# Last squares of an RMS norm: summed on VectorE, or as extra products on TensorE

## Chip, cores and metric

The kernel runs on one NeuronCore of one Trainium2 chip. The metric is device time in microseconds (us) of one launch. Three runs of the kernel before took 983.26, 982.51 and 980.66 us, so the median is 982.51 us.

## What is computed

The reference is a block of two layers on 256 tokens of width 1024. Each layer has an RMS norm, one wide projection, three kinds of attention, gated branch projections, an output projection, a second RMS norm, an MLP of width 4096, a third RMS norm and a gated projection of a side input. What matters here is the norm and where its result goes:

```python
def rmsnorm(x, g):
    xf = x.astype(jnp.float32)
    y = xf * lax.rsqrt(jnp.mean(xf * xf, axis=-1, keepdims=True) + EPS)
    return (y * g.astype(jnp.float32)).astype(x.dtype)
...
        h = rmsnorm(x, attn_norm[i])
        proj = h @ w_in[i]
...
        hm = rmsnorm(x, mlp_norm[i])
        x = x + jnp.square(jax.nn.relu(hm @ w_up[i])) @ w_down[i]

        hp = rmsnorm(x, ple_norm[i])
        x = x + jax.nn.sigmoid(hp @ w_ple_gate[i]) * (p[i] @ w_ple_proj[i])
```

## The kernel before

**Layout.** The residual `xT` lies transposed: 128 features on the partitions, 8 feature tiles, 256 tokens along the row. Each fp32 operand of a large product is split into a high and a low part (`split`, L458, for activations; `load_unit`, L393, for weights: a copy on ScalarE gives `wh`, a subtraction on VectorE or GpSimd gives `wl`), and TensorE forms three products per tile (`mm3`, L412). Weights arrive in units of 512 KB through the one queue of SyncE; a unit's buffer `w` comes free, and the next load is issued, when its `wl` has been made.

**The norm.** `class Norm` (L483) works on `xT` as its tiles are finished, two feature tiles at a time. `add` (L495) writes the two parts `xh`, `xl` of x times the gain, and has ScalarE square the two tiles into `sq`. The squares are summed over the feature tiles into one tile `ssum` (128 features by 256 tokens): GpSimd (POOL) does that for the first three pairs, VectorE (DVE) for the last pair, in two additions that follow each other (L509). `end` (L511) sums over the 128 partitions on TensorE (PE): for each of the two blocks of 128 tokens, one product with `ssum` as the 128x128 stationary operand and a column of -1 as the moving one, into `nps`. Then DVE makes `ms` (mean plus epsilon), POOL takes the power -1/2 (`rsq`), and where a row form is wanted (`row`, L522) DVE builds a diagonal `dg`, PE spreads it over the partitions (`rps`) and ScalarE (ACT) copies it to `rrow`. The large products on the unnormalised `xh`, `xl` do not wait for any of this: only what evacuates them from PSUM does, since rstd is applied there.

There are five norms that take this path (the very first sums otherwise). In the order of time: the MLP norm of layer 0 (the **first** in what follows), its gate norm (`ple`, the **second**), the attention norm of layer 1 (the **third**), the MLP norm of layer 1 (the **fourth**) and its gate norm (the **fifth**).

**The order of the work.** Nothing is issued directly. `Program` records every operation with its dependences, a cost from a table (`price`, L171) and a priority, which is the running sum of TensorE's costs where the operation was written, minus a lead for loads and weight splits. `schedule` (L218) then plays a list scheduler over the five engines on these estimates and writes down one order per engine; the chip runs each engine's list strictly in that order. All instructions therefore carry L293, the line that emits them. A new operation or another cost can shift the order of anything behind it. An engine that reaches an instruction whose input is not there yet waits, with everything behind it.

PSUM tiles of the large products, `mmp`, have two buffers; `nps` and `rps` come from another pool.

Of the kernel before, what the change touches and what calls it, by code (L numbers as in the profile page):

```python
# [18 lines left out]
OP = mybir.AluOpType  # L19
# [4 lines left out]
P = 128  # L24
# [272 lines left out]
def hybrid_block(ctx: ExitStack, tc: tile.TileContext, I, out):  # L297
    nc = tc.nc
    prog = Program(nc)
    V, S, G, T, Q = (prog.engine(e) for e in ("DVE", "ACT", "POOL", "PE", "SP"))  # L300
# [24 lines left out]
    def t2k(name, cols=512):  # L325
        return prog.tile(sp, [P, cols], F32, name, tag="t2", bufs=T2, ahead=AHEAD_T2)
# [4 lines left out]
    def small(name, shape, bufs, dt=F32, tag=None):  # L331
        return prog.tile(gaps.get(name) or pool_for(shape, dt), shape, dt, name, tag=tag or name, bufs=bufs)
# [10 lines left out]
    def trp(name):  # L343
        return prog.tile(ptr, [P, 512], F32, name, tag="tr", bufs=2, ahead=1)
# [42 lines left out]
    def mm(out, lhsT, rhs, start, stop):  # L387
        T.matmul(out=out, lhsT=lhsT, rhs=rhs, start=start, stop=stop, skip_group_check=True)
# [61 lines left out]
    def rsqrt_mean(ss, n, width):  # L450

        ms = small("ms", [P, 8], 4)
        V.tensor_scalar(ms[:, :n], ss, 1.0 / width, EPS, op0=OP.mult, op1=OP.add)
        r = small("rsq", [P, 8], 10)
        G.tensor_tensor(out=r[:, :n], in0=ms[:, :n], in1=half[:, :n], op=OP.pow)
        return r[:, :n]

    def split(src, dh, dl, col=None):  # L458

        if col is None:  # L460
            S.activation(dh, src, AF.Copy)
            V.tensor_tensor(out=dl, in0=src, in1=dh.bitcast(F32), op=OP.subtract)
        else:
            S.activation(dh, src, AF.Copy, scale=col)
            V.scalar_tensor_tensor(dl, src, col, dh.bitcast(F32), op0=OP.mult, op1=OP.subtract)
# [17 lines left out]
    class Norm(Acts):  # L483
# [11 lines left out]
        def add(self, ft, square=True):  # L495
            xh, xl = self.tiles[0]
            for f in range(ft.start, ft.stop):
                split(xT[:, f, :], xh[:, f, :], xl[:, f, :], self.gains[:, f:f + 1])
            if not square:
                return  # L500
            n = ft.stop - ft.start
            sq = t2k("sq", n * SEQ).rearrange("p (f t) -> p f t", t=SEQ)
            S.activation(sq, xT[:, ft, :], AF.Square)
            if self.ss is None:
                self.ss = small("ssum", [P, SEQ], 1)
                G.tensor_tensor(out=self.ss, in0=sq[:, 0, :], in1=sq[:, 1, :], op=OP.add)
            else:
                for f in range(n):
                    (V if ft.stop == 8 else G).tensor_tensor(out=self.ss, in0=self.ss, in1=sq[:, f, :], op=OP.add)  # L509

        def end(self, ss=None):  # L511
            if ss is None:
                ps = trp("nps")
                for b in range(NB):
                    mm(ps[:, b:b + 1], self.ss[:, b * P:(b + 1) * P], negone[:, 0:1], True, True)
                r = rsqrt_mean(ps[:, 0:NB], NB, -D)
            else:
                r = rsqrt_mean(ss, NB, D)
            self.rstd = [r[:, b:b + 1] for b in range(NB)]
# [66 lines left out]
    for n in range(2):  # L586
        for b in range(NB):
            ps = trp("xps")
# [59 lines left out]
    negone = negone_r.bitcast(F32)  # L648
# [50 lines left out]
    for l in range(DEPTH):  # L699
# [362 lines left out]
        for b in range(NB):  # L1062
            ps = trp("plps")
# [73 lines left out]
```

## Time and profile before

| what | value |
|---|---|
| runs | 983.26, 982.51, 980.66 us; median 982.51 |
| profiled execution, device time | 980.81 us |
| its span, first to last instruction | 979.0 us |
| TensorE busy | 964.5 us (99%) |
| VectorE busy | 654.6 us (67%) |
| ScalarE busy | 539.1 us (55%) |
| GpSimd busy | 154.8 us (16%) |
| DMA engines busy | 55% |
| mean granted TensorE clock | 0.996 of full |

The profiled execution's span lies 1.8 us below its device time. TensorE is the engine that is never idle for long; the others are shown with their busy time only, and much of it lies beside TensorE's. A matmul's row gives a start and a modelled duration, and these overlap: what a product costs TensorE is the distance from its start to the next start, not its duration. A plain fp32 product (`nps`, `rps`) has two matmul rows, each with a weight load of its own.

### The profile page before, as it was taken

The page shows a single profiled execution, that of the slowest core. Times are in us where ns is not written, and L with a number is a line of the kernel's source. Part 1 is how long each engine was busy: PE and PEld are TensorE (multiplying, and loading weights), DVE is VectorE, ACT ScalarE, POOL GpSimd, SP SyncE. Part 2 cuts the span into 40 slices and gives each one's busy share as a digit, 9 for nine tenths or more (in the row PEclk, how much of TensorE's full clock was granted, in tenths as well). Part 3 has the DMA queues.
Part 4 walks back from the last instruction along what each step waited for, and adds up shares of the span by engine and source line. Part 5 has one row for each costly group of instructions (what it writes and reads, how often), then busy time and mean ns, then how long its engine had stood idle before and what let it go on. Part 6 is the DMA issues. An engine that isn't in the chain of part 4 may idle for free.

```text
span 979.0 us, 18465 instructions
## 1 busy us (share of the span) xinstructions
PE 964.5 (99%) x7506; PEld 909.6 (93%) x7506; DVE 654.6 (67%) x1009; ACT 539.1 (55%) x770; POOL 154.8 (16%) x137
## 2 busy tenths in 40 slices
PE   8899999999999999999999999999999999999998
PEld 7888889889999999999989888898899999999997
DVE  8748897664777554567676599975547855565573
ACT  7437674466456444556474576645745644555462
POOL 1202122314220000001312112231151200000010
PEclk9999999999999999999999999999999999999999
DMA  8664255535666656556455543556265665566651
GB/s 282 177 207 129 89 156 172 177 114 180 197 174 198 204 183 210 176 175 214 142 171 173 190 138 110 155 170 195 88 185 182 182 214 187 172 198 201 205 173 44
DMA packets 89195, 168.59 MB, mean 172 GB/s; under 512 B 5723, under 2 KB 9237, under 8 KB 89109
## 3 DMA queue, kind: packets, MB, share of 16 engines
q1 hardware_dynamic: 89108, 167.40, 55.0%
q8 instruction: 59, 0.97, 0.4%
q14 instruction: 28, 0.22, 0.1%
HBM read 166.33 MB, written 1.05 MB: 171 GB/s over the span
## 4 chain that ended last, share of the span: by engine, by line
PE 92%; DVE 3%; ACT 2%; DMA 2%; issue 1%; SPq 0%; POOL 0%; ACTq 0%; DVEq 0%
PE mmp L293 66%; PE acc L293 18%; PE z L293 2%; PE sc L293 2%; PE oc L293 1%; DMA w<-in_w_in 1%; DVE qo L293 1%; PE qps L293 1%; ACT wh L293 1%; DVE wl L293 1%; PE ob L293 1%; PE pps L293 1%; DVE io L293 1%; DMA xin<-in_x 0%; DVE rm L293 0%
## 5 line engine op out<-in xcount | busy, mean ns | idle before, releaser
L293 ACT ACTIVATE wh<-w 128x1024 fp32r<-128x1024 f32 (+2 forms) x318 | 330.9, 1045 | 204.7 <-PE mmp L293 103.4
L293 DVE TENSOR_TENSOR wl<-w,wh 128x1024 fp32r<-128x1024 f32 (+1 forms) x284 | 342.3, 1213 | 148.1 <-ACT wh L293 143.1
L293 PE MATMUL mmp<-xh,wh 128*128 128x256 f32 x1088 | 306.4, 282 | 2.6 <-DVE rm L293 2.6
L293 PE MATMUL mmp<-xh,wl 128*128 128x256 f32 x1088 | 305.5, 281 | 0.0
L293 PE MATMUL mmp<-xl,wh 128*128 128x256 f32 x1088 | 304.6, 280 | 0.0
L293 PEld LDWEIGHTS mmp<-xh,wh 128*128 128x128 f32 x1088 | 206.5, 190 | 4.9 <-ACT wh L293 3.5
L293 PEld LDWEIGHTS mmp<-xh,wl 128*128 128x128 f32 x1088 | 206.0, 189 | 1.2 <-issue 1.0
L293 PEld LDWEIGHTS mmp<-xl,wh 128*128 128x128 f32 x1088 | 205.7, 189 | 0.4
L293 PE MATMUL acc<-yh,wh 128*128 128x256 f32 x512 | 141.5, 276 | 0.0
L293 PE MATMUL acc<-yh,wl 128*128 128x256 f32 x512 | 141.3, 276 | 0.0
L293 PE MATMUL acc<-yl,wh 128*128 128x256 f32 x512 | 141.3, 276 | 0.0
L293 POOL TENSOR_TENSOR wl<-w,wh 128x1024 fp32r<-128x1024 f32 x34 | 84.1, 2473 | 214.7 <-ACT wh L293 214.7
L293 PE MATMUL mmp<-wh,xh 128*128 128x512 f32 (+2 forms) x296 | 113.2, 382 | 0.7 <-ACT av L293 0.7
L293 PE MATMUL mmp<-wh,xl 128*128 128x512 f32 (+2 forms) x296 | 112.9, 383 | 0.2 <-DVE xl L293 0.2
L293 PE MATMUL mmp<-wl,xh 128*128 128x512 f32 (+2 forms) x296 | 112.1, 380 | 0.0
L293 PEld LDWEIGHTS acc<-yl,wh 128*128 128x128 f32 x512 | 96.1, 188 | 0.0
L293 PEld LDWEIGHTS acc<-yh,wh 128*128 128x128 f32 x512 | 96.1, 188 | 0.0
L293 PEld LDWEIGHTS acc<-yh,wl 128*128 128x128 f32 x512 | 96.1, 188 | 0.0
L293 PE MATMUL mmp<-yl,wh 128*128 128x256 f32 x336 | 93.0, 278 | 0.2
L293 PE MATMUL mmp<-yh,wh 128*128 128x256 f32 x336 | 93.0, 277 | 0.2 <-ACT pp L293 0.2
L293 PE MATMUL mmp<-yh,wl 128*128 128x256 f32 x336 | 92.8, 277 | 0.0
L293 POOL TENSOR_TENSOR rsq<-ms,half 128x8 f32<-128x8 f32 (+3 forms) x30 | 47.0, 1570 | 221.4 <-DVE ms L293 221.4
(196 smaller groups left out, 1205.1 us busy)
## 6 DMA issues: line engine op xcount, KB each, us to landing
w<-in_w_in SPq DMA_DIRECT2D x118, 512.0 KB, 3.9
w<-in_w_up SPq DMA_DIRECT2D x64, 512.0 KB, 3.8
w<-in_w_down SPq DMA_DIRECT2D x64, 512.0 KB, 4.6
w<-in_w_out SPq DMA_DIRECT2D x16, 512.0 KB, 4.4
w<-in_w_ple_gate SPq DMA_DIRECT2D x16, 512.0 KB, 3.8
w<-in_w_br_a SPq DMA_DIRECT2D x8, 512.0 KB, 4.8
w<-in_w_br_c SPq DMA_DIRECT2D x8, 512.0 KB, 3.7
w<-in_w_br_b SPq DMA_DIRECT2D x8, 512.0 KB, 4.5
```

The costliest lines, as they stand in the source:

```text
L293: getattr(self.engines[op.eng], op.name)(*op.args, **op.kw)
```

## The change

`add` keeps the squares of the last two feature tiles as they are, in `rest`, and no longer adds them to `ssum`. `end` makes three products per block of tokens in place of one, accumulated in PSUM: one of `ssum`, and one of each kept square.

```diff
             S.activation(sq, xT[:, ft, :], AF.Square)
-            if self.ss is None:
+            if ft.stop == 8:
+                self.rest = [sq[:, f, :] for f in range(n)]
+            elif self.ss is None:
                 self.ss = small("ssum", [P, SEQ], 1)
                 G.tensor_tensor(out=self.ss, in0=sq[:, 0, :], in1=sq[:, 1, :], op=OP.add)
             else:
                 for f in range(n):
-                    (V if ft.stop == 8 else G).tensor_tensor(out=self.ss, in0=self.ss, in1=sq[:, f, :], op=OP.add)
+                    G.tensor_tensor(out=self.ss, in0=self.ss, in1=sq[:, f, :], op=OP.add)
 
         def end(self, ss=None):
             if ss is None:
                 ps = trp("nps")
+
+                parts = [self.ss, *self.rest]
                 for b in range(NB):
-                    mm(ps[:, b:b + 1], self.ss[:, b * P:(b + 1) * P], negone[:, 0:1], True, True)
+                    for i, q in enumerate(parts):
+                        mm(ps[:, b:b + 1], q[:, b * P:(b + 1) * P], negone[:, 0:1], i == 0, i == len(parts) - 1)
                 r = rsqrt_mean(ps[:, 0:NB], NB, -D)
```

Over the five norms DVE loses 10 additions and PE gains 20 products (40 matmul rows). The scheduler also moves what stands near. Three pieces show it.

On PE at the second norm (`mmp_952` and `mmp_953` are products of the gate's side projection, `nps_937` the norm's sum, lines with + are of the change):

```order
 L293 MATMUL mmp_952<-yl_917,wh_950 128x256
 L293 MATMUL mmp_952<-yh_916,wl_951 128x256
+L293 MATMUL nps_937<-negone_r_130,sq_936 128x1 x2
+L293 MATMUL nps_937<-negone_r_130,ssum_927 128x1
+L293 MATMUL nps_937<-negone_r_130,sq_936 128x1 x2
 L293 MATMUL mmp_953<-yh_916,wh_950 128x256
 L293 MATMUL mmp_953<-yl_917,wh_950 128x256
 L293 MATMUL mmp_953<-yh_916,wl_951 128x256
 L293 MATMUL mmp_953<-yh_916,wh_950 128x256
-L293 MATMUL nps_937<-negone_r_130,ssum_927 128x1 x2
```

The sum stands four products earlier, ahead of `mmp_953`; its first product, of `ssum` for the first block, is not in this piece and stands eight products further ahead.

On DVE at the second norm (`ssum_927` the additions, `ms_938` and `dg_940` the steps behind the sum, `wl_977` and `wl_980` splits of later weights):

```order
 L293 TENSOR_TENSOR xT_102<-acc_685,xT_102 128x512
 L293 SCALAR_TENSOR_TENSOR xl_915<-xT_102,ncol_101,xh_914 128x256
-L293 TENSOR_TENSOR ssum_927<-ssum_927,sq_936 128x256 x2
+L293 TENSOR_SCALAR ms_938<-nps_937 128x2
 L293 SCALAR_TENSOR_TENSOR xl_915<-xT_102,ncol_101,xh_914 128x256 x2
-L293 TENSOR_SCALAR ms_938<-nps_937 128x2
+L293 TENSOR_SCALAR dg_940<-ident_87,rsq_939 128x128 x2
 L293 TENSOR_TENSOR wl_977<-w_975,wh_976 128x1024
-L293 TENSOR_SCALAR dg_940<-ident_87,rsq_939 128x128 x2
 L293 TENSOR_TENSOR wl_980<-w_978,wh_979 128x1024
```

The two additions are gone, and `ms` stands in their place, ahead of the two `xl`; `dg` passes one weight split.

On PE at the third norm (`mmp_1011` and `mmp_1013` are the two blocks of the first projection of layer 1, `nps_993` the sum):

```order
+L293 MATMUL nps_993<-negone_r_130,sq_992 128x1 x2
+L293 MATMUL nps_993<-negone_r_130,ssum_971 128x1
+L293 MATMUL nps_993<-negone_r_130,sq_992 128x1 x2
 L293 MATMUL mmp_1011<-wh_1009,xl_955 128x512
-L293 MATMUL mmp_1013<-wh_1006,xh_954 128x512
-L293 MATMUL mmp_1013<-wl_1007,xh_954 128x512
-L293 MATMUL mmp_1013<-wh_1006,xl_955 128x512
-L293 MATMUL nps_993<-negone_r_130,ssum_971 128x1 x2
 L293 MATMUL mmp_1013<-wh_1009,xh_954 128x512
```

The group of five products stands one product of `mmp_1011` and six of `mmp_1013` ahead of the next tile, `mmp_1030`; before, the sum stood six products ahead of it. The first product of `ssum` stands four products of `mmp_1011` ahead of the group.

At the first and the fourth norm the first product of `ssum` stands 39 products of 256 columns ahead of where the sum stood, and the other five 23 products ahead of it, with the 16 between them. At the fifth the first stands two products into `mmp_1803`, with the sum ten products and eight transposes behind that place before; the other five stand six products of `mmp_1804` ahead of the old place, and four of the eight transposes move to a later tile.

## Rows read from the trace of the kernel before

**Rows 1.** The page: TensorE's busy time; shares of the chain that ended last.

```profile
PE 964.5 (99%) x7506; PEld 909.6 (93%) x7506; DVE 654.6 (67%) x1009; ACT 539.1 (55%) x770; POOL 154.8 (16%) x137
...
PE 92%; DVE 3%; ACT 2%; DMA 2%; issue 1%; SPq 0%; POOL 0%; ACTq 0%; DVEq 0%
```

**Rows 2.** Tile ssum: count, duration in ns (min/median/max), first and last start.

```profile
L293 PE MATMUL nps<-negone_r,ssum x20: 164/250/271, 293.2 to 951.8; 128*128 128x1 f32 x20
L293 DVE TENSOR_TENSOR ssum<-ssum,sq x10: 410/418/1709, 290.7 to 950.0; 128x256 f32<-128x256 f32 x10
```

**Rows 3.** Timeline of PE, first norm: start, duration, instruction, [idle before <-releaser].

```profile
293.03 0.28 PE L293 MATMUL mmp<-xh,wh 128*128 128x256 f32 x1
293.15 0.50 PE L293 MATMUL nps<-negone_r,ssum 128*128 128x1 f32 x4
...
293.71 0.28 PE L293 MATMUL mmp<-xh,wl 128*128 128x256 f32 x1
```

**Rows 4.** Timeline of PE, second norm.

```profile
465.99 0.28 PE L293 MATMUL mmp<-yl,wh 128*128 128x256 f32 x1
...
467.68 0.28 PE L293 MATMUL mmp<-yh,wh 128*128 128x256 f32 x1
469.01 0.61 PE L293 MATMUL nps<-negone_r,ssum 128*128 128x1 f32 x4 [1.06 <-DVE ssum L293]
...
469.68 0.36 PE L293 MATMUL mmp<-yh,wl 128*128 128x256 f32 x1
...
473.22 0.28 PE L293 MATMUL mmp<-xl,wh 128*128 128x256 f32 x1
...
473.90 0.59 PE L293 MATMUL rps<-dg,negone_r 128*128 128x256 f32 x2
474.15 0.47 PE L293 MATMUL mmp<-xl,wh 128*128 128x256 f32 x1
```

**Rows 5.** Timelines of POOL, ACT and DVE, second norm.

```profile
464.08 1.79 POOL L293 TENSOR_TENSOR ssum<-ssum,sq 128x256 f32<-128x256 f32 x2 [2.10 <-ACT sq L293]
465.83 2.39 POOL L293 TENSOR_TENSOR wl<-w,wh 128x1024 fp32r<-128x1024 f32 x1
469.90 1.63 POOL L293 TENSOR_TENSOR rsq<-ms,half 128x2 f32<-128x2 f32 x1 [1.68 <-DVE ms L293]
...
466.07 0.62 ACT L293 ACTIVATE sq<-xT 128x512 f32<-128x512 f32 x1
...
466.79 2.17 DVE L293 TENSOR_TENSOR ssum<-ssum,sq 128x256 f32<-128x256 f32 x2 [1.52 <-ACT sq L293]
```

**Rows 6.** Stretches: busy time by engine, then granted TensorE clock, DMA share, GB/s.

```profile
32.80:36.20 3.40, 3.40 (x19) 3.40 (x18) 2.24 (x8) 0.00 (x0) 0.55 (x1) 0.50 0.77 243
...
469.70:473.10 3.40, 3.40 (x18) 3.40 (x18) 2.56 (x6) 1.54 (x2) 1.63 (x1) 0.51 0.66 194
...
517.20:520.60 3.40, 3.40 (x30) 3.34 (x30) 2.83 (x9) 1.36 (x3) 0.00 (x0) 1.00 0.61 177
```

**Rows 7.** Timeline of PE: its two other waits of over one microsecond.

```profile
32.02 0.36 PE L293 MATMUL mmp<-xh,wh 128*128 128x256 f32 x1 [2.56 <-DVE rm L293]
...
517.04 0.33 PE L293 MATMUL ips<-ident,io 128*128 128x128 f32 x1 [1.62 <-DVE io L293]
```

**Rows 8.** Timelines of PE and DVE, third norm.

```profile
503.32 0.39 PE L293 MATMUL mmp<-wh,xh 128*128 128x512 f32 x1
...
504.70 0.50 PE L293 MATMUL nps<-negone_r,ssum 128*128 128x1 f32 x4
505.06 0.48 PE L293 MATMUL mmp<-wh,xh 128*128 128x512 f32 x1
...
506.95 0.41 PE L293 MATMUL mmp<-wh,xh 128*128 128x324 f32 x1 [0.26 <-ACT av L293]
...
505.23 0.16 DVE L293 TENSOR_SCALAR ms<-nps 128x2 f32<-128x2 f32 x1 [0.69 <-PE nps L293]
```

**Rows 9.** Timeline of POOL, first norm: its last additions, and the power behind the sum.

```profile
286.79 1.79 POOL L293 TENSOR_TENSOR ssum<-ssum,sq 128x256 f32<-128x256 f32 x2 [5.64 <-ACT sq L293]
293.93 0.71 POOL L293 TENSOR_TENSOR rsq<-ms,half 128x2 f32<-128x2 f32 x1 [5.35 <-DVE ms L293]
```

## Prediction

> **What bounds the kernel now.** I read the page first, to see who is never idle: TensorE (PE) is busy 964.5 of 979.0 us and holds 92% of the chain that ended last [rows 1]. What lies on PE therefore lengthens the run by its full price unless PE would have waited there anyway, and what is taken from VectorE (DVE, 67%) is worth only the wait of PE that it ends. Then I read PE's timeline around each of the five norms for waits. At the first norm there is none: the sum's products stand in an unbroken stream [rows 3]. The fourth and the fifth look the same. At the second, PE stands idle for the additions of DVE [rows 4], and the timelines of the other engines say why [rows 5]. At the third it does not wait for the sum, but a little later for what follows it [rows 8]. A table of stretches gives the clock [rows 6].
>
> **What a product costs.** In the steady stream a product of 256 columns starts 0.113 us after the one before it (473.22 to 473.90 holds six steps) [rows 4]. From 293.03 to 293.71 PE starts one such product, the four matmul rows of two `nps` products, and one more large one [rows 3]. That is 0.68 us, less 2 x 0.113 leaves 0.454, so **0.227 us** per `nps` product, or 0.113 per matmul row. One column costs as much as 256, because each row loads 128 columns of weights. The Trainium skill would price it lower: "TensorE: Matmul & The Clock Gate", section "Back-to-back issue gap", gives matmuls of 1 to 64 columns a floor of about 25 ns; at that, the 40 added rows would be an estimated 1.0 us. The measured row decides.
>
> **First, fourth and fifth norm: +0.91 us each.** Four more products by 0.227 are 0.91, and nothing is there to be won. New waits could come in two places. The first product, of `ssum`, now stands 39 products earlier than the sum did, so PE reaches it at 293.15 - 39 x 0.113 = 288.73, and POOL's last addition ends at 286.79 + 1.79 = 288.58 [rows 3, 9]: 0.15 us to spare, and I price it at nothing. If that cover is gone, each 0.1 us of lateness is 0.1 us of PE. The squares' own products stand another 16 products later. The two additions that DVE loses are 0.42 us each in ten places [rows 2]; behind them DVE splits weights and makes `ms`, on none of which PE waits here, so they are worth nothing. Moving `rps` and `rrow` forward brings no gain either, since the evacuation that uses them holds up no product. Together: +2.73.
>
> **Second norm: a gain, of a size that hangs on the clock.** ACT finishes the squares at 466.69. The first DVE addition starts at 466.79 and both end only at 468.96: POOL is splitting weights from 465.83 to 468.22, and the addition, 0.42 us elsewhere, takes up to 1.71 [rows 2, 5]. PE, whose last product started at 467.68, goes on at 469.01 [rows 4]. In the change the sum needs only the squares and POOL's additions. The first product would start at 465.99 (POOL ends at 464.08 + 1.79 = 465.87) [rows 4, 5]; eight products later, at 465.99 + 0.23 + 8 x 0.113 = 467.12, the squares have been ready for 0.4 us, and the other five run to 468.26. Work that PE does there also covers a short wait for a PSUM buffer before `mmp_953`.
>
> Before, the stretch from 465.99 to 474.15 holds 37 large products, the sum and `rps`: 8.16 us [rows 4]. After, it should hold 37 x 0.113 = 4.19, six `nps` products at 0.227 = 1.36, `rps` 0.25 (473.90 to 474.15), in all 5.80, plus a possible wait for `rps`. That one I bound: `ms` about 0.17 us after the last product and the power 0.24 after that, as at the first and third norm, so it starts at 468.67 and lasts 0.71 (DVE quiet) to 1.63 (DVE busy beside it) [rows 5, 9]; with 0.5 for `dg`, `rps` can run at 469.9 to 470.8, and PE is there at 468.26 + 18 x 0.113 = 470.3. So 0 to 0.5; I take 0.2, nearer the short one, since DVE has only two `xl` there. The stretch becomes 6.0: **-2.16**.
>
> Of this, 1.61 is clock: from 469.68 to 473.22 PE started 17 products in 3.54 us, at twice the usual step (17 x 0.113 = 1.93), and the stretch shows a granted clock of 0.51, the 1.2 GHz level [rows 4, 6]. It fell behind the wait. It also fell behind a wait of 2.56 us at 32.02 (0.50 after it), and not behind one of 1.62 us at 517.04 (1.00 after it) [rows 6, 7]. A wait of 1.06 and some idling before it is thus at the edge, and one execution doesn't say whether the others paid the 1.61. The price in the median run lies between 0 and 1.61; the longer wait that cost no clock is the nearest row, so I take 0.5. The second norm is then -0.55 - 0.5 = **-1.05**.
>
> **Third norm: +0.77.** A product of 512 columns steps by 0.23 (503.32 to 504.70 holds six) [rows 8]. The first `nps` product takes the place of a large one that now follows, so the group of five starts at about 504.70 and ends at 505.83. `mmp_1030` needs a PSUM buffer that ACT evacuates with the new rstd. From the sum's last row (before: next product at 505.06) to `ms` (505.23) are 0.17 us, and from there over POOL and ACT to `mmp_1030` (506.95) 1.72 [rows 8]. That gives 505.83 + 0.17 + 1.72 = 507.72 against 506.95: +0.77. PE arrives at 505.83 + 7 x 0.23 = 507.44, so part of the added work falls into a wait that was there already. The reordered steps of ACT and DVE ahead of this norm only bring the squares earlier; I price them at nothing, with 0.3 either way.
>
> **Sum.** 2.73 - 1.05 + 0.77 = **+2.45 us**, on the median of 982.51: **984.96**. Against the profiled execution's own time, where the clock did fall, it is 2.73 - 2.16 + 0.77 = +1.34, 982.15 from 980.81, which itself is 1.7 below the median. With no clock to win back it is +2.95. A measurement of this kernel tells about 0.3%, 2.95 us, from no change, so the forecast is "same", leaning slow.
>
> **Rivals.**
> - *New waits take the place of the old one* (slower, 30%). The wait for DVE becomes waits on POOL: for its additions, which now gate a product 39 places earlier with 0.15 us to spare, and for the power at the second norm (0.5 in place of 0.2). It decides once POOL's additions end after PE's arrival. For it: the thin cover. Against it: the same additions end at the same distance in the fourth norm. With the runs' clock unfallen before (2.95), 0.3 at `rps` and 0.2 to 0.5 at two or three norms, it is +3.65 to +4.75: 986.2 to 987.3. The unfallen clock with no new wait at all ends on the bound, and I count a third of its cases here.
> - *The new bursts lower the clock* (slower, 7%). Five one-column products are 1.13 us in which PE streams ten columns. If the chip takes that for idling, a fall costs 1.61 as at the second norm; at two to five norms that makes +5.7 to +10.5, 988.2 to 993.0. Against it: two such products in a row leave the next steps at 0.113 [rows 3]; bursts of five are not in the trace. The section on what is happening in the skill's page "TensorE: Matmul & The Clock Gate" ties the clock to how busy PE has been, without saying how one column counts; no row here shows it.
> - *Every execution before paid for the clock, and the chains move up* (faster, 3%). All of 1.61 comes back, which leaves +1.34; and the sum at the first norm ends at 288.73 + 0.23 + 16 x 0.113 + 1.13 = 291.9, 1.7 us earlier than at 293.6 [rows 3]. If PE waited on what follows at three norms, that would be another -5.1: -3.8, 978.7. Against it: no wait of PE hangs on these chains but those priced.
> - *A product at its issue floor* (2%): the added 4.54 us shrink to 1.0 and the sum is -1.1, still within 0.3%. The section cited above states that floor; rows 3 speak against it.
>
> **How the numbers follow.** Forecast 58% (+1.2 to +2.95), new waits 30%, bursts 7%, faster 3%, issue floor 2%. Faster by over 0.3%: 0.03. Within: 0.58 + 0.02 = 0.60. Slower: 0.37. The range goes from 982.0 (the profiled sum) to 987.6 (the waits at their full price and some tenths of spread); the bursts are left out.
>
> **What would show it.** DVE 10 additions fewer, about 4 us less busy; 60 `nps` matmul rows in place of 20, still at 0.113 a step. At the second norm no idle time of PE on DVE and a clock of 1.00 throughout. At the third `mmp_1030` still waiting some 0.3 us for ACT's `av`. Wrong would be: idle time of PE in front of an `nps` product with POOL or ACT as the releaser, a stretch at 0.5 behind a burst, or PE standing still elsewhere because the new order came out late.

## The result, and the profile after

The change makes the kernel slower: a median of 990.12 us over 8 runs (984.63 to 995.21) against 979.94 of the kernel before, run beside it on the same chip (8 runs, 977.81 to 983.26). The ratio is 1.0098, with a 95% interval of 1.0071 to 1.0125. The forecast was 984.96 with a range that ended at 987.6, so the time lies outside, on the slow side. It stood on 982.51, the median of the first three runs of the kernel before; of the change itself it gave +2.45 us, and +10.2 was measured. The runs of the changed kernel spread over 10.6 us, those of the kernel before over 5.5. Its profiled execution happens to be the fastest of the eight: 984.63 us, span 982.9.

The page of the changed kernel: busy time and the chain that ended last, to be read against [rows 1].

```profile
PE 967.9 (98%) x7546; PEld 913.0 (93%) x7546; DVE 648.7 (66%) x999; ACT 540.0 (55%) x770; POOL 155.0 (16%) x137
...
PE 92%; DVE 3%; DMA 1%; ACT 1%; issue 1%; POOL 0%; SPq 0%; ACTq 0%; DVEq 0%
```

PE has the 40 matmul rows that were announced, DVE 10 instructions and 5.9 us less. The tiles `nps` and `ssum` of the changed kernel (count, duration in ns as min/median/max, first and last start):

```profile
L293 PE MATMUL nps<-negone_r,sq x40: 164/250/250, 290.7 to 953.6; 128*128 128x1 f32 x40
...
L293 PE MATMUL nps<-negone_r,ssum x20: 165/250/250, 288.7 to 953.1; 128*128 128x1 f32 x20
...
L293 DVE TENSOR_SCALAR ms<-nps x5: 159/159/160, 291.9 to 953.8; 128x2 f32<-128x2 f32 x5
```

So the work is as priced [rows 2], and 40 rows at some 0.113 us are 4.5 us. At the second norm the wait for DVE is gone too. PE there, in the changed kernel:

```profile
468.08 0.50 PE L293 MATMUL nps<-negone_r,sq 128*128 128x1 f32 x4
468.44 0.36 PE L293 MATMUL nps<-negone_r,ssum 128*128 128x1 f32 x2
468.67 0.58 PE L293 MATMUL nps<-negone_r,sq 128*128 128x1 f32 x4
469.12 0.36 PE L293 MATMUL mmp<-yh,wh 128*128 128x256 f32 x1
...
471.26 0.59 PE L293 MATMUL rps<-dg,negone_r 128*128 128x256 f32 x2
```

No idle time stands in front of the sum (1.06 before [rows 4]), and the clock of the same stretch is at its upper level (2.4 GHz), 1.00 where it was 0.51 [rows 6]:

```profile
469.70:473.10 3.40, 3.40 (x30) 3.35 (x29) 3.19 (x6) 1.94 (x4) 0.71 (x1) 1.00 0.51 160
```

Set side by side product for product, this one pair of executions (+3.8 us) divides as follows. Each number says by how much more the changed kernel lags, at the same large products, behind the place than ahead of it.

| place | expected | found |
|---|---|---|
| first norm | +0.91 | +0.95 |
| second norm, clock included | -2.16 | -2.35 |
| third norm | +0.77 | +1.74 |
| two stretches away from any norm (524 to 560, 749 to 771) | 0 | +0.85, +0.81 |
| fourth, fifth norm | +0.91 each | +0.96, +0.88 |
| the start of the kernel | 0 | -0.06 |

The norms account for +2.2. Two things are new here, the third norm and two stretches in which nothing was changed; and the other 5 to 10 us, which most executions pay and this one doesn't, are not in this trace at all. The next section looks for them.

### The profile page after: what moved, and what is told of

It reads as the page before. It is cut to its first block, busy times and chain, and to the rows that moved or that the text cites. A ratio compares the mean times of both kernels' runs of the same rounds, so it can differ in the third digit from the quotient of the medians.

```text
span 982.9 us, 18539 instructions
## 1 busy us (share of the span) xinstructions
PE 967.9 (98%) x7546; PEld 913.0 (93%) x7546; DVE 648.7 (66%) x999; ACT 540.0 (55%) x770; POOL 155.0 (16%) x137
## 4 chain that ended last, share of the span: by engine, by line
PE 92%; DVE 3%; DMA 1%; ACT 1%; issue 1%; POOL 0%; SPq 0%; ACTq 0%; DVEq 0%
PE mmp L293 66%; PE acc L293 18%; PE z L293 2%; PE sc L293 2%; DMA w<-in_w_in 1%; PE oc L293 1%; DVE qo L293 1%; PE qps L293 1%; ACT wh L293 1%; DVE wl L293 1%; PE ob L293 1%; PE nps L293 1%; PE pps L293 1%; DVE io L293 1%; DVE rm L293 0%
```

## The experiments

**The change again, twice** (no edit).

> The change once more, unaltered, for a second profile. Pace theory: large products of 256 columns start every 113.3 or every 117.8 ns, and which of the two is settled at each fp32 product in between and then holds; behind the first and the fourth norm 1388 of them follow without another, so the slow pace costs 1388 x 4.5 ns = 6.2 us per layer. Then an execution near 990 us shows one of these two stretches at 117.8, one near 985 none, one near 995 both, and no idle time of TensorE that the profile at 982.9 us lacks. New-waits theory: an execution near 990 shows 5 to 8 us of idle time in front of nps or rps products, and 113.3 in both stretches. Clock theory: it shows stretches at a granted clock of 0.5 behind the bursts of five products.

> As the one before it, a third profile of the change: pace theory, a time of about 984, 990 or 996 us with none, one or both of the long stretches at 117.8 ns; the others, idle time or a lowered clock in the place of that.

The first took 988.89, 994.37, 994.40 and 994.56 us (ratio 1.0134, 1.011 to 1.0158), the second, a single run, 988.62. Their profiled executions (spans of 987.1 and 986.9) show what the one above lacks. The view is busy time by stretch (columns as in [rows 6]) for a piece inside each MLP, 300 to 450 and 784 to 930 us; the figure behind PE's busy time is the number of its products. Kernel before:

```profile
300.00:450.00 150.00, 150.00 (x1326) 150.00 (x1325) 85.85 (x87) 74.60 (x85) 0.00 (x0) 1.00 0.63 197
784.00:930.00 146.00, 146.00 (x1291) 146.00 (x1290) 83.45 (x84) 72.78 (x82) 0.00 (x0) 1.00 0.62 196
```

The change, profiled execution of the result:

```profile
300.00:450.00 150.00, 150.00 (x1326) 150.00 (x1325) 86.38 (x87) 75.21 (x86) 0.00 (x0) 1.00 0.63 198
784.00:930.00 146.00, 146.00 (x1290) 146.00 (x1290) 83.85 (x85) 73.47 (x85) 0.00 (x0) 1.00 0.62 197
```

The change, first of the two repeats:

```profile
300.00:450.00 150.00, 150.00 (x1326) 150.00 (x1325) 85.76 (x86) 74.63 (x85) 0.00 (x0) 1.00 0.63 198
784.00:930.00 146.00, 146.00 (x1242) 146.00 (x1241) 79.29 (x80) 70.73 (x80) 0.00 (x0) 1.00 0.59 187
```

In the repeat the second MLP gets through 1242 products where it was 1290, with PE busy all the time, no waits, and the granted clock at 1.00: 146 us / 1242 is 117.6 ns per product, 150 / 1326 is 113.1. In the second repeat it is the first MLP (1276 products) and not the second (1291). **PE has two steps for the same product stream, 113.3 and 117.8 ns, and an MLP of 1388 products in an unbroken stream costs 1388 x 4.5 ns = 6.2 us more at the long one.** That is the missing size: neither, one or two MLPs at the long step. (In what follows, a group of products *turns* the step when it leaves the other one than it met.)

Where the step is set shows PE's timeline in the same repeat, which has both outcomes. First norm, then fourth:

```profile
288.06 0.30 PE L293 MATMUL nps<-negone_r,ssum 128*128 128x1 f32 x2
...
289.01 0.28 PE L293 MATMUL mmp<-xl,wh 128*128 128x256 f32 x1
...
290.03 0.28 PE L293 MATMUL mmp<-xl,wh 128*128 128x256 f32 x1
290.14 0.50 PE L293 MATMUL nps<-negone_r,sq 128*128 128x1 f32 x4
...
291.49 0.28 PE L293 MATMUL mmp<-xl,wh 128*128 128x256 f32 x1
...
293.85 0.28 PE L293 MATMUL mmp<-xh,wh 128*128 128x256 f32 x1
293.97 0.60 PE L293 MATMUL rps<-dg,negone_r 128*128 128x256 f32 x2
...
770.32 0.29 PE L293 MATMUL nps<-negone_r,ssum 128*128 128x1 f32 x2
...
770.78 0.28 PE L293 MATMUL mmp<-xh,wh 128*128 128x256 f32 x1
...
772.31 0.28 PE L293 MATMUL mmp<-xl,wh 128*128 128x256 f32 x1
772.43 0.50 PE L293 MATMUL nps<-negone_r,sq 128*128 128x1 f32 x4
...
774.14 0.28 PE L293 MATMUL mmp<-xl,wh 128*128 128x256 f32 x1
...
776.07 0.28 PE L293 MATMUL mmp<-xh,wh 128*128 128x256 f32 x1
776.18 0.59 PE L293 MATMUL rps<-dg,negone_r 128*128 128x256 f32 x2
```

At the first norm the products behind the early rows of `ssum` keep the short step (289.01 to 290.03: nine steps of 113 ns), those behind the group of ten rows have the long one (291.49 to 293.85: 20 of 118), and behind `rps` the MLP runs short. At the fourth it is the other way round: long behind the early rows (770.78 to 772.31: 13 of 118), short behind the ten (774.14 to 776.07: 17 of 114), long behind `rps`. So a plain fp32 product in the stream can turn the step, and what it leaves lasts until the next interruption. In the kernel before there are two such places per MLP norm, `nps` and `rps`. PE there:

```profile
294.06 0.28 PE L293 MATMUL mmp<-xh,wl 128*128 128x256 f32 x1
...
295.60 0.28 PE L293 MATMUL mmp<-xh,wh 128*128 128x256 f32 x1
295.71 0.60 PE L293 MATMUL rps<-dg,negone_r 128*128 128x256 f32 x2
```

Behind `nps` the long step (294.06 to 295.60: 13 of 118), 18 products that cost nothing worth counting, and behind `rps` the short one for the whole MLP.

**The change at the MLP norms alone, and at the other three alone.** `tail` turns the new form on per norm; where it is off, the old additions stand.

```diff
-            if ft.stop == 8:
+            if ft.stop == 8 and self.tail:
...
-        norm = mlp = Norm(ncol[:, 16 + 8 * l:24 + 8 * l])
+        norm = mlp = Norm(ncol[:, 16 + 8 * l:24 + 8 * l], tail=False)
```

These are the lines of the second kernel; the first has `tail=False` at the second, third and fifth norm instead.

> The change at the first and the fourth norm alone (8 of the 20 added products). Pace theory: the loss is here, since only these two norms stand ahead of the long stretches: 1.8 us for the products plus 0, 6.2 or 12.4 us by execution, so a median 6 to 9 us above before and a spread of several us. New-waits theory: about 2 us of products plus at most 1 us of waits, 2 to 3 us above before with little spread. Clock theory: two of the five bursts, so about 2 x 1.6 + 1.8 = 5 us, in every execution alike.

> The change at the second, third and fifth norm alone. Pace theory: at most 2 us either way of before, and no wider spread than before, since no long stretch follows these norms. New-waits theory: most of the 10 us is here, since the reordered products and waits of the second and third norm are. Clock theory: three of the five bursts, 3 x 1.6 + 2 = 7 us above before.

MLP norms alone: 993.66 us (987.26 to 995.84; ratio 1.0125, 1.0098 to 1.0153). The other three: 981.61 (979.91 to 982.67; ratio 1.0013, 1.0004 to 1.0022). The whole loss comes from the first and the fourth norm, where the sum added four products at 0.23 us. The profiled execution of the MLP norms alone (994.17) has both MLPs at the long step:

```profile
300.00:450.00 150.00, 150.00 (x1276) 150.00 (x1275) 83.05 (x84) 72.75 (x83) 0.00 (x0) 1.00 0.60 188
784.00:930.00 146.00, 146.00 (x1242) 146.00 (x1241) 79.88 (x81) 70.64 (x80) 0.00 (x0) 1.00 0.60 188
```

**One, two, and a pair of unread products in the kernel before.**

```diff
             nxt = up(c)
+            if c == 1:
+                mm(trp("dmy")[:, 0:1], ident, negone[:, 0:1], True, True)
             down(c - 1, hs)
```

Two apart have the same lines again behind `down`; the pair has the `mm` twice in a row.

> The kernel before, unchanged but for one product per layer whose result nobody reads (128x128 constants against one column, two matmul rows). It stands 230 products ahead of the MLP norm's sum. Theory of the pace: TensorE starts products of 256 columns every 113.3 or every 117.8 ns; each interruption by plain fp32 products whose operands are ready changes from the one to the other, and what stands behind it keeps the new one until the next interruption. One more interruption ahead of the norm turns all that follows: slow up to the sum (230 x 4.5 ns = 1.0 us), fast for the 2.6 us to the spread of rstd, slow for the 1370 products of the MLP (6.2 us). With 0.23 us for the product that is 7.4 us per layer, about +14.9 in all, so about 995, in every execution. Rival (work and waits): an added product costs its own time alone, and the change lost its time to late operands and to the new order: then +0.45, about 980.3.

> The same product per layer, and a second one like it 220 products into the MLP. Theory of the pace: slow from the first one to the sum (1.0 us) and from the spread of rstd to the second one (220 x 4.5 ns = 1.0 us), fast from there on: with 0.45 us for the two products 2.4 us per layer, +4.9 in all, about 985. Twice as much is added as with one, and it should cost a third. Rival (work and waits): +0.9, about 980.8, and never less than with one product.

> The same two products per layer as in the kernel with two, but next to each other, at the place of the first. Theory of the pace: two products in a row are one interruption, as the norm's own two are, so it goes as with one product and costs +0.9 for the products and +14.4 for the slow stretches, about 995. Rival (work and waits): +0.9, about 980.8, the same as with the two apart. If each product counts by itself, they cancel: also +0.9.

Measured: one 980.40 (ratio 1.0004, 0.9989 to 1.0018), two 980.37 (1.0005, 0.9988 to 1.0022), the pair 981.31 (1.0014, 1.0003 to 1.0025). All three forecasts of the pace theory were wrong by up to 15 us, and the traces say why: all six MLPs run at the short step. The theory's first form, that any such interruption turns the step, is false. The pair does leave the long step behind it (231 products at 117.8 ns up to the norm, both times), the lone one sometimes does; but the norm's own `nps` group of four rows leaves the long step whatever it meets: long to long as well as short to long. From there `rps` makes it short. The group of `nps` in the kernel before **wipes out** what came ahead, and in every trace of a kernel that keeps it at the MLP norms, `rps` left the short step behind it.

**The whole change, the sum's products in another order: six in one group.**

```diff
-                parts = [self.ss, *self.rest]
+                parts = [*self.rest, self.ss]
```

> The whole change, with the products of one block added up in another order: the two kept squares first, ssum last. All six products of a sum then become ready together and stand in one group at each of the five norms, 23 products ahead of the old place at the MLP norms, and nothing waits for GpSimd. The work of every engine is that of the change. Theory of the pace: two interruptions per MLP norm, as in the kernel before, so both MLPs run at 113.3 ns in every execution; what is left is 1.8 us for the two MLP norms and the 1.3 to 1.7 us that the other three cost by themselves: about 983, with runs that agree within some 3 us, against 988 to 995 of the change. Rival (work and waits): if the price of the added products or the new order of the splits makes the time, it is the change's own, 988 to 994; if it is only the first product's wait for GpSimd (0.15 us per norm), 0.3 less than the change.

981.72 us (979.40 to 983.87; ratio 1.0012, 1.0000 to 1.0025). The same products, additions and splits as in the change, in an order that has no early product, take 8 us off; no other line was touched. Both MLPs run at the short step:

```profile
300.00:450.00 150.00, 150.00 (x1326) 150.00 (x1325) 85.22 (x86) 74.17 (x86) 0.00 (x0) 1.00 0.63 198
784.00:930.00 146.00, 146.00 (x1291) 146.00 (x1290) 83.07 (x84) 73.33 (x83) 0.00 (x0) 1.00 0.63 196
```

This kills the rival that prices and waits of the added products made the loss.

**One more spread like `rps`, and two more, in the kernel before.** The second kernel has the same product once more, some 210 products later.

```diff
         mlp.end()
         mlp.row
+        mm(trp("dmy")[:, 0:SEQ], negone, mlp.made_row[:, 0, :], True, True)
```

> The kernel before, with one product more per layer whose result nobody reads: a second spread like rps (plain fp32, 256 columns, two matmul rows), 8 products behind rps. The theory of the pace as the traces so far leave it: a group of two one-column products (four rows) leaves the slow step of 117.8 ns behind it, whichever was there before; a product like rps changes the step, from slow to fast and from fast to slow; whatever stands, stays until the next plain product. So the second spread should turn the 1360 products of each MLP slow, in every execution: 2 x (1360 x 4.5 ns + 0.44 for the product) = +13.1, about 993. Rival (only waits and prices count): +0.9, about 981. Rival (the pace of an MLP hangs on the early product of the change and its wait for GpSimd alone): also +0.9.

> The same, and a third spread 218 products into the MLP. Theory of the pace: it changes the step back to fast, so only 210 products per layer are slow: 2 x (210 x 4.5 ns + 0.88) = +3.7, about 984; the more work is added, the less it costs. Rivals: +1.8, about 982, and never less than with one spread.

994.04 us with one (992.20 to 995.23; ratio 1.0127, 1.0108 to 1.0145), 984.21 with two (983.36 to 985.88; ratio 1.0035, 1.0023 to 1.0046): the theory's 993 and 984, where prices gave 981 and 982. An unread product of 0.4 us per layer costs 14 us, and a second one gives 10 back. With one, the MLPs of its profiled execution:

```profile
300.00:450.00 150.00, 150.00 (x1276) 150.00 (x1275) 82.19 (x83) 72.74 (x83) 0.00 (x0) 1.00 0.60 187
784.00:930.00 146.00, 146.00 (x1241) 146.00 (x1240) 78.96 (x80) 70.64 (x82) 0.00 (x0) 1.00 0.61 188
```

In a kernel that is otherwise the one before, with no change to a norm, this is the loss of the change, made on purpose. That the step of the MLP's stream costs these microseconds is shown.

**The whole change in a third order: both products of `ssum` early.**

```diff
-                for b in range(NB):
-                    for i, q in enumerate(parts):
-                        mm(ps[:, b:b + 1], q[:, b * P:(b + 1) * P], negone[:, 0:1], i == 0, i == len(parts) - 1)
+                for i, q in enumerate(parts):
+                    for b in range(NB):
+                        mm(ps[:, b:b + 1], q[:, b * P:(b + 1) * P], negone[:, 0:1], i == 0 and b == 0, i == len(parts) - 1)
```

> The whole change with the sum's products in a third order: ssum of both blocks first, then the four of the kept squares. At the MLP norms four rows stand at the early place (39 products ahead of where the sum stood before) and eight at the later one, where the change has two and ten and the joined order none and twelve; the work is the same in all three. Theory of the pace: four rows leave slow, eight change slow to fast (ten did so, from slow), rps changes fast to slow: both MLPs slow in every execution, 12.4 us above the joined order, about 994, with runs that agree within some 3 us. If the wait for GpSimd at the early place still decides it by execution: 982 to 994, spread as the change's. Rival (only waits and prices count): as the change or 0.3 less.

982.38 us (981.90 to 984.76; ratio 1.0019, 1.0008 to 1.0031): a miss of 12 us for the theory as it stood, and another gain over the change from an order of the same products. In the traces DVE, ACT and POOL do the same instructions in the same order as in the change. The four early rows left the long step at the first norm, but the short one at the fourth. The group of eight did not turn the step as the ten rows do; it left the long one whatever came ahead (long to long at the first norm, short to long at the fourth), like the four rows of `nps`. Groups of four, eight and twelve rows wipe out (but for these four early rows at the fourth norm), the ten turn.

**The new form at the second norm alone, in the joined order.** `tail` as above, on where `l == 0` in the gate norm, and `parts` as in the joined kernel.

> The change at the second norm alone, in the joined order; the other four norms as before. There the wait of PE for DVE's additions goes and nothing else does: -1.05 by the prediction (-0.55 without the clock, -2.2 where the clock had fallen), so 978 to 979.5. The MLPs are as before in either theory. If the three norms ahead of and behind it had cost the change nothing by themselves, it would be 0.

978.76 us (977.25 to 980.87; ratio 0.9980, 0.9967 to 0.9994), 1.6 below the kernel before. Only about half of that is the wait for DVE. In all seven profiled executions with the old form at this norm, `rps` left the long step behind it; here it left the short one, and the 166 large products up to the third norm take 19.04 us in place of 19.78. That is 0.74 us which neither the prediction nor the expectation counted. This version beats both kernels.

**The early product later, by 6 and by 7 places.** A lead of -3.3 (or -3.4) on the first product of `ssum`, at the two MLP norms; nothing else moves on any engine.

```diff
                     for i, q in enumerate(parts):
+                        prog.lead = -3.3 if self.late and i == b == 0 else 0.0
                         mm(ps[:, b:b + 1], q[:, b * P:(b + 1) * P], negone[:, 0:1], i == 0, i == len(parts) - 1)
+                prog.lead = 0.0
```

> The whole change, with one thing moved: the early product of ssum (two rows) at the two MLP norms stands 6 products later, 0.7 us, where GpSimd's additions have been done for some 0.8 us in place of 0.15. The group of ten rows, all else and the order of every other engine are the change's. Theory A (the thin cover of the wait for GpSimd makes the early rows' outcome vary): with the operand ready the outcome is one and the same; as the two lone unread products with ready operands and no long row left the fast step both times, it should be fast, so both MLPs fast in every execution: about 982 to 984, runs within some 3 us. (If it is always slow instead, about 995, as narrow.) Theory B (it varies whether the operand is ready or not): as the change, 983 to 995 with the spread of its runs, median 988 to 994.

> The same, 7 products later in place of 6, so that another product of the three of a tile follows. Theory A: again one outcome in every execution, the same as with 6 if the place among the three doesn't matter: 982 to 984 (or about 995). Theory B: 983 to 995, spread.

With 6: 989.46 us (984.97 to 991.63; ratio 1.0078, 1.0049 to 1.0106). With 7: 995.08 (992.15 to 996.13; ratio 1.0136, 1.0116 to 1.0156). GpSimd's additions were done 0.83 to 1.07 us ahead of the early rows. In all four norms of the two traces these rows turned the step: long to short once, short to long three times. With the operand ready, then, the three groups of a norm (two rows, ten, `rps`) all turn, and the MLP gets the opposite of what came in. With 6 the step came in long at the first norm, so the first MLP was short and the second long; with 7 it came in short both times, and both MLPs were long. Neither theory had that whole: in these two traces the outcome of the early rows doesn't vary, but the step ahead of them does.

Where that variation comes from, the changed kernel's own trace shows. PE and its weight loads (PEld) ahead of the fourth norm, in the profiled execution of the result:

```profile
749.50 0.28 PE L293 MATMUL mmp<-yh,wh 128*128 128x256 f32 x1
749.90 0.39 PE L293 MATMUL mmp<-yl,wh 128*128 128x256 f32 x1
...
749.89 0.19 PEld L293 LDWEIGHTS mmp<-yl,wh 128*128 128x128 f32 x1 [0.32 <-DVE yl L293]
```

PE waits here for DVE's `yl`, 0.40 us from start to start; the short step before it becomes the long one. The kernel before has the same wait at 266.45 and at 748.37, and left it with the short step both times. PE there, the second time:

```profile
748.37 0.28 PE L293 MATMUL mmp<-yh,wh 128*128 128x256 f32 x1
748.77 0.38 PE L293 MATMUL mmp<-yl,wh 128*128 128x256 f32 x1
748.99 0.29 PE L293 MATMUL mmp<-yh,wl 128*128 128x256 f32 x1
```

Leaving out the kernels with an unread one-column product at this place, the sixteen profiled executions hold 26 such waits. The step came in short at all of them and went out long at 4. At this wait the step is drawn anew, and only a group that wipes out keeps the draw from the MLP. This is the stretch from 749 us on in the table of the result. The other one begins behind two products `ips` of 128 columns at 524.26, which left the long step in the changed kernel and the short one in the kernel before.

## Why the prediction was wrong

**What every trace bears out.** Counted over all sixteen profiled executions, in the stream of 256-column products (at least eight of them on either side) and not right behind a wait: a spread of one product (`rps` and its unread copies) turned the step 44 times of 44. The ten rows of the changed sum turned it 12 times of 12. Groups of four, eight or twelve one-column rows left the long step 25 times of 26. The two early rows turned it in 10 of 12; the two misses were both in the change itself, with 0.14 us between the end of GpSimd's additions and the row. The one miss of the groups, the four early rows, had 0.15. But four other early places with 0.15 us did turn the step; with 0.36 us and more all six did. Right behind a wait the rule of the groups does not hold: behind the old form's wait at the second norm, four rows left the short step in all five executions in which the clock stayed up. Of the 12 MLPs behind an early product, 5 ran at the short step and 7 at the long one, and in all 12 the step ahead of the ten rows decided it. Lone unread one-column products are less regular: they turned the step in 2 of 6, and four of these stood at the wait for `yl`. Of the profiled executions with an early product at the MLP norms, the one with no long MLP took 984.6, those with one 988.6 to 991.0, and those with two 994.2 to 994.9.

**Point by point.**

- *"In the steady stream a product of 256 columns starts 0.113 us after the one before it."* This is the step that failed, by what it took for granted. Rows 4 and 3 show 0.113, and I made it the price of every large product in every stretch, so that a sum's products could only cost their own time. The trace of before held the other step too: its products between `nps` and `rps` run at 118 ns, a line away from rows that I quoted. "First, fourth and fifth norm: +0.91 us each ... nothing is there to be won" was right for the products (+0.95, +0.96, +0.88) and put what they leave behind them at nothing, without a reason: 6.2 us for each MLP that comes out long, as 7 of the 12 behind an early product did. Two of the listed signs of being wrong did not come, idle time in front of an `nps` row and a stretch at half the clock behind a burst; the step was not on the list.
- *0.227 us per `nps` product*: right. The one-column rows step by 0.112. The Trainium skill, "TensorE: Matmul & The Clock Gate", section "LDWEIGHTS (loading the stationary operand)", puts a load of 128 columns at 128 / 1.2, an estimated 107 ns, which this agrees with. In the same page of the Trainium skill, the section "Back-to-back issue gap" gives its floor of 25 ns for isolated matmuls; for a stream of weight loads and matmuls it says that both set the spacing. I had read that floor as a price of these rows. Its gap for 256 columns, N / 2.4 + 2.5, an estimated 109 ns, is for an isolated matmul too. The runs show 113.3 and 117.8 in one kernel at one clock, and the choice between them was worth more than all the added products.
- *Second norm*: right in its mechanism. Expected -2.16 where the clock had fallen, found -2.35. How often it falls I had left open, and the seven profiled executions with the old form there show it: behind waits of 1.03 to 1.06 us the granted clock fell to about half in two and stayed at 1.00 in five. From one large product ahead of the sum to the 64th behind it, PE took 11.6 us where the clock fell, 9.9 to 10.0 where it didn't, and 9.2 to 9.3 in the new form. So without the clock the wait was worth 0.6 to 0.8, where I had 0.55; the clock's 1.6 was paid in two of the seven, where I took 0.5 for the median run.
- *Third norm, +0.77*: wrong by a factor of two, +1.74. I took the 1.72 us from `ms` to `mmp_1030` over from before. In the changed kernel that chain is longer; POOL, DVE, ACT and PE there:

```profile
504.84 1.63 POOL L293 TENSOR_TENSOR rsq<-ms,half 128x2 f32<-128x2 f32 x1 [4.76 <-DVE ms L293]
...
504.68 1.23 DVE L293 TENSOR_TENSOR wl<-w,wh 128x1024 fp32r<-128x1024 f32 x1
...
506.50 0.69 ACT L293 ACTIVATE av<-mmp,rsq 128x512 f32<-128x512 f32 x1 [3.19 <-POOL rsq L293]
...
507.24 0.41 PE L293 MATMUL mmp<-wh,xh 128*128 128x324 f32 x1 [0.96 <-ACT av L293]
```

  In the kernel before, the power took 0.71 us, and DVE began its weight split when it was nearly done:

```profile
505.47 0.71 POOL L293 TENSOR_TENSOR rsq<-ms,half 128x2 f32<-128x2 f32 x1 [5.19 <-DVE ms L293]
...
506.04 1.23 DVE L293 TENSOR_TENSOR wl<-w,wh 128x1024 fp32r<-128x1024 f32 x1 [0.64 <-ACT wh L293]
```

  Now the split starts right behind `ms` (at 504.68) and lies beside the power, which takes 1.63 us. I had bounded the power by just these two values at the second norm, where it took 0.88, and not at the third, where the order of DVE had changed as well.
- *Rival "new waits"* (30%): its place was right, its mechanism not. The early product of `ssum` is what does the harm, and GpSimd's additions do end 0.15 us ahead of it, as worked out; but PE hardly waits. Moving the product to where the cover is wide made it no better.
- *Rival "the new bursts lower the clock"* (7%): the time fell into its range, 988.2 to 993.0, for another reason. The granted clock is 1.00 in every MLP at either step.
- *Luck*: the profiled execution of the change, 984.63 us, lies 0.3 us from the forecast. But against the profiled execution of the kernel before, the prediction gave +1.34 and +3.8 was found.

What stays open is why, in a norm, an odd number of plain products (one or five) turns the step and an even one (two, four, six) leaves the long one, why lone unread products often did nothing, and what in TensorE holds the step; no run here looks inside. Nor is it shown what decides the draw at the wait for `yl`.

## What to carry to other kernels

Where a kernel is bound by one long uniform stream, divide a long stretch by its count of products in every stage and execution before pricing an edit: a step that differs by 4% over a thousand products outweighs any handful of added ones. When an edit costs more than its instructions, and differs from run to run with no waits to show for it, compare the step behind each interruption of the stream. Keep small products of another kind in one group at one place, and prefer the order whose outcome doesn't hang on what came before: here the same six products took 982 us joined and 990 split.

## What the runs showed of the hardware

- 128x256 fp32r products with a weight load each stream at 113.3 or at 117.8 ns, at the same granted clock of 1.00 (1326 or 1276 of them in the same 150 us), and keep to the one or the other for 150 us and more.
- The step is set where plain fp32 products, a short operand wait (0.40 us from start to start) or two products of 128 columns interrupt the stream; about five large products behind it the new step stands.
- In seven executions, behind a wait of 1.03 to 1.06 us of TensorE, the granted clock fell to about half in two and stayed at 1.00 in five.
- An unread spread of two matmul rows per layer made the kernel 14 us slower; a second one per layer took 10 us of that back.
